# First tiles of a hybrid encoder step: statistics on TensorE, fewer and larger loads, another split of the first h

## The chip, the cores and the metric

The kernel runs on one core of one Trainium2 chip, as one launch that takes every input from device memory and writes every output there. The metric is device time in microseconds (us); lower is better. TensorE (PE) multiplies matrices, VectorE (DVE) and GpSimd (POOL) do elementwise work, ScalarE (ACT) does functions of one operand, and SyncE (SP) issues all DMA transfers of this kernel from one queue.

## The reference

One layer of a streaming encoder over 2048 prompt positions and 32 sample positions, width 1024, in float32. The part that the change touches is its beginning, for the first 512 positions:

```python
cs = jax.nn.silu(c)
mod = (cs @ ada_w[l] + ada_b[l])[:, None, :]
sh1, sc1, gt1, sh2, sc2, gt2 = jnp.split(mod, 6, axis=-1)
h = rmsnorm(x, norm_mix_g[l]) * (1 + sc1) + sh1
p = h @ w_in                      # columns for u, v, q, k, vv, z, a, b
...
x = x + gt1 * (concat(mixer A, mixer B) @ w_out)
h = rmsnorm(x, norm_ffn_g[l]) * (1 + sc2) + sh2
x = x + gt2 * (jnp.square(jax.nn.relu(h @ w_up[l])) @ w_down[l])
y = rmsnorm(x, final_norm_g)
```

`rmsnorm(x, g)` is x times the power -0.5 of (mean of squares over the 1024 channels + 1e-6), times g. There are two condition vectors c (prompt and sample), so `mod` has two columns. Mixer A is a gated MLP over chunks of 128 positions, for whose `v` columns the second stage of the kernel computes a gelu; mixer B is a gated delta rule.

## The kernel before

Channels lie on the 128 partitions, in KT = 8 tiles k; positions lie along the free dimension, in two halves and, in the first half, in two groups g of 512. A float32 product is made of three matmuls: each operand is split into a high part (ACT copies it to a rounded type) and a low part (DVE subtracts), and high*high, low*high and high*low are added in PSUM (`mm3`). `BH[k]`, `BL[k]` are the parts of h; `wh`, `wl` those of a slab of weights (1 MB, loaded as two halves into raw buffers, `slab`). There are two pairs wh/wl, so slab n+2 takes the place of slab n.

**The first stage** is `startup` (L645). It loads c and the eight tiles of x for group 0, squares them on ACT, adds the squares on DVE (`stats`), and makes the row of factors r in `rms_row` (L779): matmuls with a column of ones sum over the partitions (the squares are the loaded weights, 128 positions at a time), DVE scales and adds epsilon, POOL raises to -0.5 with `pow`, PE transposes back into a row over all partitions (in PSUM bank tag "M", one bank), and ACT copies the row to SBUF. Then it goes over k. `ada_first(k)` (L727) loads two transfers of 512 KB of `ada_w` for this tile of channels (ring "ada" of four buffers in the slots 0 to 3), multiplies them with silu(c) in eight small groups of matmuls that end as partial sums on eight rows, copies these to SBUF on ACT, transposes them on PE (two transposes), and adds the four parts and the bias on DVE, one instruction after the other; one more DVE instruction makes a1 = (1+scale)*g. `h_tile` multiplies x by r (DVE, or POOL where k % 3 is 2), applies a1 and the shift (DVE, POOL or ACT by k) and splits the result. Then four heads' z products take this k (`gemm_k`, `mm3` with 512 columns): heads 0, 1 from slab 1, heads 2, 3 from slab 2, each in a PSUM bank over all eight k (bank tags "g", "g", "g", "L").

After the last k, `z_out` (L1038) puts silu(z) of head h into the next buffer of ring "Q" and stores it to `z_d`. Ring "Q" is the halves of the slots 18, 19, 20, in that order: the four heads use 18 low, 18 high, 19 low, 19 high. Then group 1 of x is loaded, summed and turned into h in the same way (`stats(1)`, `h_tile`), and slab 3 (`w_v`, first part) is set going.

**The second stage** is `v_stage` (L936). It first calls `next_slab`, which sets slab 4 (`w_v`, second part) going; then `v_tile` (L953) for the chunks 0 to 3 with slab 3, and for the same chunks with slab 4. A `v_tile` is 24 matmuls of 260 columns into a bank of ring "g" (three banks), then a gelu on ACT into the next buffer of ring "va": (18, 0), (18, 256), (18, 512), (18, 768), (19, 0) and on. The raw buffers of the slabs 1 to 4 are `raws`: the tile `wr0` and slot 6, in turn.

The order of all instructions on all engines is not written by hand: every operation goes into a `Program` (L203) with a cost and its dependencies by memory region, and `schedule` (L239) plays a list schedule over six engines (DMA is one of them) and emits the instructions in the order of their planned starts. Each engine then runs its instructions strictly in that order, and semaphores enforce the dependencies. What has the earlier due GEMM goes first (`due`). `after` in the change adds a dependency to this plan.

At the very end `final` (L1772) calls `rms_row` with three rows of squares for the last group: the sum so far, and those of tiles 6 and 7.

Of the kernel before, what the change touches and what calls it, by code (L numbers as in the profile page):

```python
# [10 lines left out]
AF = mybir.ActivationFunctionType  # L11
ALU = mybir.AluOpType
# [4 lines left out]
P = 128  # L17
D = 1024
KT = 8
# [171 lines left out]
def R(x):  # L191
    return x.ap if isinstance(x, View) else x
# [132 lines left out]
class Kern:  # L325
# [61 lines left out]
    def dma(self, out, in_, n=None):  # L387
# [4 lines left out]
        self.p.op(DMA, max(500, x), lambda: nc.sync.dma_start(out=R(out), in_=R(in_)), [out], [in_], lat=DMA_LATENCY + min(0, x - 500))  # L392

    def mms(self, calls, cost):

        nc = self.nc

        def fn():
            for out, l, r, kw in calls:
                nc.tensor.matmul(R(out), R(l), R(r), **kw)  # L400

        shape = (calls[0][1].shape[0], calls[0][1].n)
        self.p.op(PE, cost, fn, [c[0] for c in calls], [x for c in calls for x in c[1:3]], table=shape)

    def mm(self, out, lhsT, rhs, cost=None, start=True, stop=True, **kw):
        c = cost or 9 + 4 * rhs.n / 2.4
# [130 lines left out]
    def setup(self):  # L537
        sb = self.sbuf
# [20 lines left out]
        rg = self.ring  # L559
        hv = lambda *ss: [(s, lo) for s in ss for lo in (0, HALF)]  # L560
# [84 lines left out]
    def startup(self):  # L645
        i, c = self.i, self.dma
        c(self.craw, i["cT"])
        self.act(self.cs, self.craw, AF.Silu)
        self.fill(self.ones, 1.0, DVE)
        self.fill(self.mhalf, -0.5, DVE)  # L650
        xr = [[8, 9, 10, 11], [4, 5, 7, 12]]
        x = [[self.slot(s, lo, (P, 512)) for s in xr[g] for lo in (0, HALF)] for g in range(2)]
        load = lambda g: [c(x[g][k], self.x_src(0)(k, 512 * g, 512)) for k in range(KT)]
        row = [self.row[:, 512 * g : 512 * g + 512] for g in range(2)]

        def stats(g):
            acc = row[g]
            self.act(acc, x[g][0], AF.Square)
            for k in range(1, KT):
                sq = self.half("E")  # L660
                self.act(sq, x[g][k], AF.Square)
                self.tt(acc, acc, sq, ALU.add, DVE if g == 0 or k % 2 else POOL)
            self.rms_row([acc], 512, acc)
# [7 lines left out]
        stats(0)  # L671
# [12 lines left out]
        for h in range(H):  # L684
            self.z_out(0, 0, h, zs[h])
        load(1)
        stats(1)
        for k in range(KT):
            self.h_tile(0, 1, k, x[1][k], row[1], self.a1, 0)
        self.next_slab()  # L690
        self.consts()

# [34 lines left out]
    def ada_first(self, f, ps):  # L727

        ws = []
        for e in range(2):  # L730
            w = self.new("ada")
            self.dma(w, self.i["ada0"][f, :, 1024 * e : 1024 * e + 1024])
            ws.append(w)
        for e in range(2):
            self.mms([(ps[32 * s : 32 * s + 2, :256], self.cs[:, 4 * e + s, :], ws[e][:, 256 * s : 256 * s + 256],
                       dict(start=(e == 0), stop=(e == 1), tile_position=(0, 32 * s), skip_group_check=True))
                      for s in range(4)], 480)
# [41 lines left out]
    def rms_row(self, acc, w, out):  # L779

        ps = self.bank("M")

        pieces = [min(e, w - P) for e in range(0, w, P)]
        n = len(pieces)
        calls = []
        for c, e in enumerate(pieces):
            for b, a in enumerate(acc):
                calls.append((ps[:, c : c + 1], a[:, e : e + P], self.ones[:, 0:1],
                              dict(start=(b == 0), stop=(b == len(acc) - 1))))
# [465 lines left out]
    def delta_chain(self, hf, h):  # L1255
        c0 = CHUNKS[hf][0]
        nch = len(CHUNKS[hf])
        S = self.S[h]
# [600 lines left out]
```

## Time and profile before

| | us |
|---|---|
| median of 3 runs | 2356.8 |
| lowest, highest | 2352.51, 2358.11 |
| the profiled execution's own time | 2357.03 |
| its span | 2355.2 |

The page of the profile gives shares over the whole span; the timeline lists instructions with start and duration in us (merged where one follows another, with a count), in brackets the idle time of the engine before it and what ended that. PEclk is the TensorE clock that the profile records as granted; 1.00 is full. A row "PEld" is the load of a stationary operand, which overlaps PE.

### The profile page before, as it was taken

The numbers are of one execution on the slowest core, as the hardware profiler recorded it, in microseconds if no ns is written. First come the engines' busy times: TensorE is split into PE (matmuls) and PEld (weight loads), VectorE is DVE, ScalarE is ACT, GpSimd is POOL, SyncE is SP. The second block draws the span as 40 slices with busy tenths as digits, with TensorE's granted clock in tenths as the row PEclk, the third lists the DMA queues.
The fourth block names the chain that finished last, engine by engine and source line by source line (L and its number), as shares of the span: only waits on it lengthen the run. The fifth ranks groups of instructions, "written<-read, shape, count | busy, mean of one in ns | idle before, by whom it ended". The sixth has DMA issues, their size and how long they took to land.

```text
span 2355.2 us, 45713 instructions
## 1 busy us (share of the span) xinstructions
PE 2304.7 (98%) x15888; PEld 2173.7 (92%) x15888; DVE 1667.3 (71%) x3675; ACT 1226.0 (52%) x2818; POOL 597.4 (25%) x827
## 2 busy tenths in 40 slices
PE   7999999999999999999999999999999999999998
PEld 4877878999999888999999999999999999999998
DVE  5556657567665546479999999877667786666775
ACT  4565646456566434366655555664433574334343
POOL 2234421412432322444444434300000050000001
PEclk9999999999999999999999999999999999999999
DMA  9698667466457767887777787998667797666771
GB/s 317 220 316 290 203 190 247 148 182 200 148 168 240 235 213 237 260 268 272 244 239 250 255 281 245 336 321 270 218 210 253 251 297 248 214 220 219 239 230 54
DMA packets 369264, 556.28 MB, mean 236 GB/s; under 512 B 71212, under 2 KB 191424, under 8 KB 369032
## 3 DMA queue, kind: packets, MB, share of 16 engines
q1 hardware_dynamic: 369032, 553.35, 72.0%
q8 instruction: 126, 2.06, 0.4%
q14 instruction: 106, 0.87, 0.1%
HBM read 398.92 MB, written 154.28 MB: 235 GB/s over the span
## 4 chain that ended last, share of the span: by engine, by line
PE 83%; DMA 6%; DVE 6%; ACT 3%; issue 2%; POOL 1%; SPq 0%; POOLq 0%; DVEq 0%; ACTq 0%
PE f L400 50%; PE g L400 24%; PE C L400 3%; DVE s L354 2%; ACT s L339 2%; PE B L400 2%; PE L L400 1%; DVE s L359 1%; DMA pk_d<-s 1%; DVE wl L354 1%; DMA s<-ada 1%; PE M L400 1%; PE L L411 1%; DVE BL L354 1%; DMA s<-xT 1%
## 5 line engine op out<-in xcount | busy, mean ns | idle before, releaser
L339 ACT ACTIVATE s<-s 128x348 fp32r<-128x348 f32 (+13 forms) x1079 | 494.8, 482 | 348.0 <-DVE s L354 136.3
L400 PE MATMUL f<-s,wh 128*128 128x348 f32 (+1 forms) x2760 | 661.4, 322 | 5.8 <-DVE s L359 2.4
L400 PEld LDWEIGHTS f<-s,wh 128*128 128x128 f32 x2760 | 479.4, 188 | 9.2 <-DVE s L354 3.5
L354 DVE TENSOR_TENSOR s<-f,s 128x348 f32<-128x348 f32 (+1 forms) x696 | 347.6, 511 | 179.3 <-PE f L400 178.3
L400 PE MATMUL f<-s,wl 128*128 128x348 f32 (+1 forms) x1380 | 443.6, 321 | 0.3 <-DVE wl L354 0.3
L400 PE MATMUL g<-BH,wh 128*128 128x512 f32 (+2 forms) x1112 | 422.6, 380 | 2.0 <-ACT BH L339 2.0
L354 DVE TENSOR_TENSOR s<-s,s 128x348 fp32r<-128x348 f32 (+7 forms) x688 | 356.0, 545 | 58.1 <-ACT s L339 24.1
L400 PE MATMUL g<-BH,wl 128*128 128x512 f32 (+2 forms) x1112 | 392.6, 353 | 0.0
L400 PE MATMUL g<-BL,wh 128*128 128x512 f32 (+2 forms) x1112 | 391.3, 352 | 0.2 <-DVE BL L354 0.2
L400 PE MATMUL f<-BL,wh 128*128 128x348 f32 (+1 forms) x1016 | 328.9, 324 | 2.2 <-DVE BL L354 2.2
L400 PE MATMUL f<-BH,wh 128*128 128x348 f32 (+1 forms) x1016 | 328.3, 323 | 1.7 <-ACT BH L339 1.7
L400 PE MATMUL f<-BH,wl 128*128 128x348 f32 (+1 forms) x1016 | 328.5, 323 | 0.0
L339 ACT ACTIVATE wh<-s 128x512 fp32r<-128x512 f32 (+1 forms) x278 | 174.0, 634 | 236.2 <-PE f L400 189.5
L354 POOL TENSOR_TENSOR s<-s,s 128x512 f32<-128x512 f32 (+5 forms) x154 | 188.7, 1233 | 304.0 <-ACT s L339 148.2
L354 POOL TENSOR_TENSOR s<-s 64x39 f32<-64x39 f32 (+12 forms) x299 | 156.7, 524 | 426.7 <-issue 381.0
L400 PEld LDWEIGHTS f<-s,wl 128*128 128x128 f32 x1380 | 259.8, 188 | 0.7 <-DVE wl L354 0.6
L400 PEld LDWEIGHTS g<-BH,wh 128*128 128x128 f32 x1112 | 211.3, 190 | 26.0 <-issue 7.8
L400 PEld LDWEIGHTS g<-BH,wl 128*128 128x128 f32 x1112 | 210.3, 189 | 19.4
L400 PEld LDWEIGHTS g<-BL,wh 128*128 128x128 f32 x1112 | 211.5, 190 | 15.2 <-DVE BL L354 0.6
L354 DVE TENSOR_TENSOR wl<-s,wh 128x512 fp32r<-128x512 f32 (+1 forms) x278 | 211.2, 768 | 19.2 <-ACT wh L339 18.9
L359 DVE SCALAR_TENSOR_TENSOR s<-s,s,s 128x128 f32<-128x128 f32 (+5 forms) x318 | 163.5, 529 | 71.9 <-ACT s L339 43.8
L354 DVE TENSOR_TENSOR wl<-wr,wh 128x512 fp32r<-128x512 f32 (+2 forms) x161 | 153.5, 956 | 63.9 <-ACT wh L339 61.1
(115 smaller groups left out, 3400.5 us busy)
## 6 DMA issues: line engine op xcount, KB each, us to landing
s<-w_u SPq DMA_DIRECT2D x124, 256.0 KB, 3.8
s<-w_d SPq DMA_DIRECT2D x118, 256.0 KB, 2.8
wh<-su_d SPq DMA_DIRECT2D x113, 256.0 KB, 3.1
wl<-su_d SPq DMA_DIRECT2D x113, 256.0 KB, 4.2
wh<-sd_d SPq DMA_DIRECT2D x108, 256.0 KB, 3.1
wl<-sd_d SPq DMA_DIRECT2D x108, 256.0 KB, 3.9
wr<-w_b SPq DMA_DIRECT2D x42, 512.0 KB, 4.7
s<-adaw SPq DMA_DIRECT2D x32, 512.0 KB, 5.7
```

Source lines behind the costliest of these rows:

```text
L339: self.p.op(ACT, c, lambda: nc.scalar.activation(out=R(out), in_=R(in_), func=func, **{k: R(v) for k, v in kw.items()}), [out, accum], [in ...
L354: self.p.op(eng, c, lambda: e.tensor_tensor(out=R(out), in0=R(a), in1=R(b), op=op), [out], [a, b])
L359: self.p.op(DVE, c, lambda: nc.vector.scalar_tensor_tensor(out=R(out), in0=R(a), scalar=R(s), in1=R(b), op0=op0, op1=op1), [out], [a, s, b])
L400: nc.tensor.matmul(R(out), R(l), R(r), **kw)
L411: self.p.op(PE, 114, lambda: nc.tensor.transpose(R(out), R(in_), R(ident)), [out], [in_, ident])
```

## The change

It alters the first stage, one shared helper and one later load:

- x comes in four transfers of 512 KB per group instead of eight of 256 KB.
- For group 0, all eight squares are kept (new ring "sq", in the slots 14, 15, 21, 22) and `rms_row` gets them as a list. `rms_row` now makes one PE operation per row of squares instead of one for all; for a single row this is what it was. DVE adds no squares for group 0, and r stays in PSUM and is read there.
- One `pow` on POOL is issued ahead of everything, its result unused.
- In `ada_first`, two matmuls with a 128x2 matrix `sel` of ones and zeros take the place of the two transposes, and sum the four parts; one DVE instruction adds the bias. `sel` is made with three DVE instructions.
- For group 0, h is made by DVE (x*r), ACT (scale and shift), and the split; POOL has no part in it.
- Ring "ada" has eight buffers: the slots 0, 1, 2, 3, 25, 26, 27, 20. `after` keeps the matmuls of `ada_first(k)` behind the GEMMs of k-3 in the plan.
- `raws` gets slots 18 and 19, ahead of slab 1: slab 1 now uses wr0 and slot 6, slab 2 slots 18 and 19, slab 3 wr0 and slot 6, slab 4 slots 18 and 19.
- The load of the sample's delta state s0, which the plan had put first of all, is kept behind the last k.

```diff
@@ setup
+        self.sel = sb("sel", [P, 2])
-        rg("ada", [(s, 0) for s in range(4)], (P, 1024))
+        rg("ada", [(s, 0) for s in (0, 1, 2, 3, 25, 26, 27, 20)], (P, 1024))
+        rg("sq", hv(14, 15, 21, 22), (P, 512))
@@ startup
+        both = [[self.slot(s, 0, (P, 2, HALF))[:, :, :512] for s in xr[g]] for g in range(2)]
+        load = lambda g: [c(both[g][e], i["xT"][2 * e : 2 * e + 2, :, 512 * g : 512 * g + 512].rearrange("k p t -> p k t"),
+                            8 * P * 512) for e in range(4)]
+        row = self.row[:, :512]
+        def stats():
+            sq = [self.half("sq") for _ in range(KT)]
+            for k in range(KT):
+                self.act(sq[k], x[0][k], AF.Square)
+            return self.rms_row(sq, 512, None)
+        self.tt(self.rcol[0], self.ones[:, :4], self.mhalf, ALU.pow, POOL)
         load(0)
...
+        self.tt(self.sel, self.ident[:, 0:2], self.ident[:, 32:34], ALU.add)
+        for e in (64, 96):
+            self.tt(self.sel, self.sel, self.ident[:, e : e + 2], ALU.add)
+        r = stats()
         self.sq = self.slab_list()
+        self.raws += [self.slot(s, 0, (P, SLABW // 2)) for s in (18, 19)]
         self.sn = self.slab(*self.sq.pop(0))
...
+        done = []
         for k in range(KT):
-            self.ada_first(k, ps[k % 2])
-            self.h_tile(0, 0, k, x[0][k], row[0], self.a1, 0)
+            self.ada_first(k, ps[k % 2], done[k - 3] if k > 2 else ())
+            t = x[0][k]
+            self.tt(t, t, r, ALU.mult)
+            self.act(t, t, AF.Identity, scale=self.a1[:, k, 0:1], bias=self.modc[:, 0, k, 0:1])
+            self.split(self.BH[k][:, :512], self.BL[k][:, :512], t)
             for h in range(H):
                 self.gemm_k(zs[h][:, :512], *z[h // 2], h % 2, 0, 0, k)
+            done.append((len(self.p.ops) - 1,))
+        self.begun = done[-1]
@@ ada_first
-            self.tr(ps[:, 256 + 128 * e : 384 + 128 * e], ar[:, 128 * e : 128 * e + 128], self.ident)
+            self.mm(ps[:, 256 + 2 * e : 258 + 2 * e], ar[:, 128 * e : 128 * e + 128], self.sel, 230)
         m = self.modc[:, 0:2, f]
-        for s in range(4):
-            part = ps[:, 256:512].re("p (e s r) -> p e s r", e=2, s=4)[:, :, s, 0:2]
-            self.tt(m, part, self.adab[:, 0:2, f] if s == 0 else m, ALU.add)
+        self.tt(m, ps[:, 256:260].re("p (e r) -> p e r", e=2), self.adab[:, 0:2, f], ALU.add)
@@ rms_row
-        self.mms(calls, 230 * len(calls))
+        for b, a in enumerate(acc):
+            self.mms([(ps[:, c : c + 1], a[:, e : e + P], self.ones[:, 0:1],
+                       dict(start=(b == c == 0), stop=(b == len(acc) - 1 and c == n - 1), skip_group_check=len(acc) > 1))
+                      for c, e in enumerate(pieces)], 230 * n)
@@ delta_chain
-                self.dma(S, self.i["s0"][h])
+                self.dma(S, self.i["s0"][h], after=self.begun)
```

The statistics of group 1 keep their old form, with the additions on DVE and POOL in turn.

More of the change, by code (lines that the diff above doesn't have):

```diff
@@ L385, in transpose32, with dma @@
         self.p.op(DVE, 68 + 1.042 * out.n, lambda: nc.vector.transpose(R(out), R(in_)), [out], [in_])
-    def dma(self, out, in_, n=None):
+    def dma(self, out, in_, n=None, after=()):
         nc = self.nc
@@ L391, in dma, with mms @@
         x = b / 360
-        self.p.op(DMA, max(500, x), lambda: nc.sync.dma_start(out=R(out), in_=R(in_)), [out], [in_], lat=DMA_LATENCY + min(0, x - 500))
-    def mms(self, calls, cost):
+        self.p.op(DMA, max(500, x), lambda: nc.sync.dma_start(out=R(out), in_=R(in_)), [out], [in_], lat=DMA_LATENCY + min(0, x - 500), after=after)
+    def mms(self, calls, cost, after=()):
         nc = self.nc
@@ L402, in mms @@
         shape = (calls[0][1].shape[0], calls[0][1].n)
-        self.p.op(PE, cost, fn, [c[0] for c in calls], [x for c in calls for x in c[1:3]], table=shape)
+        self.p.op(PE, cost, fn, [c[0] for c in calls], [x for c in calls for x in c[1:3]], table=shape, after=after)
     def mm(self, out, lhsT, rhs, cost=None, start=True, stop=True, **kw):
@@ L652, in startup @@
         x = [[self.slot(s, lo, (P, 512)) for s in xr[g] for lo in (0, HALF)] for g in range(2)]
[L653 to L663, printed above, removed]
+        both = [[self.slot(s, 0, (P, 2, HALF))[:, :, :512] for s in xr[g]] for g in range(2)]
[8 more added lines that the diff above has]
+        self.tt(self.rcol[0], self.ones[:, :4], self.mhalf, ALU.pow, POOL)
         load(0)
@@ L670, in startup @@
         self.cp(self.ident, k1[:, 120:248])
-        stats(0)
+        self.tt(self.sel, self.ident[:, 0:2], self.ident[:, 32:34], ALU.add)
+        for e in (64, 96):
+            self.tt(self.sel, self.sel, self.ident[:, e : e + 2], ALU.add)
+        r = stats()
         self.sq = self.slab_list()
+        self.raws += [self.slot(s, 0, (P, SLABW // 2)) for s in (18, 19)]
         self.sn = self.slab(*self.sq.pop(0))
@@ L686, in startup @@
         load(1)
-        stats(1)
+        self.act(row, x[1][0], AF.Square)
+        for k in range(1, KT):
+            sq = self.half("E")
+            self.act(sq, x[1][k], AF.Square)
+            self.tt(row, row, sq, ALU.add, DVE if k % 2 else POOL)
+        self.rms_row([row], 512, row)
         for k in range(KT):
-            self.h_tile(0, 1, k, x[1][k], row[1], self.a1, 0)
+            self.h_tile(0, 1, k, x[1][k], row, self.a1, 0)
         self.next_slab()
@@ L725, in consts, with ada_first @@
                 self.dma(self.pk_d[h][8][:, :, :P], zero.re("p (a b) -> p a b", a=3))
-    def ada_first(self, f, ps):
+    def ada_first(self, f, ps, after=()):
         ws = []
@@ L736, in ada_first @@
                        dict(start=(e == 0), stop=(e == 1), tile_position=(0, 32 * s), skip_group_check=True))
-                      for s in range(4)], 480)
+                      for s in range(4)], 480, after)
         ar = self.arow[:, 256 * (f % 2) : 256 * (f % 2) + 256]
@@ L784, in rms_row @@
         n = len(pieces)
[L785 to L789, printed above, removed]
-        self.mms(calls, 230 * len(calls))
+        for b, a in enumerate(acc):
+            self.mms([(ps[:, c : c + 1], a[:, e : e + P], self.ones[:, 0:1],
+                       dict(start=(b == c == 0), stop=(b == len(acc) - 1 and c == n - 1), skip_group_check=len(acc) > 1))
+                      for c, e in enumerate(pieces)], 230 * n)
         r = self.rcol[0]
```

## Prediction, made before the changed kernel ran

> **What bounds the kernel now.** I read the page first, then the timeline of PE over the first 62 us, then that of the other engines, then the windows in which the clock fell.
>
> ```profile
> span 2355.2 us, 45713 instructions
> PE 2304.7 (98%) x15888; PEld 2173.7 (92%) x15888; DVE 1667.3 (71%) x3675; ACT 1226.0 (52%) x2818; POOL 597.4 (25%) x827
> ```
>
> ```profile
> 12.64 1.87 PE L400 MATMUL M<-ones,s 128*128 128x1 f32 x8 [12.64 <-DVE s L354]
> 14.44 2.17 PE L400 MATMUL C<-s,s 128*2 128x256 f32 x16
> 16.78 1.12 PE L411 MATMUL M<-ident,rcol 128*128 128x128 f32 x4 [0.17 <-POOL rcol L354]
> ...
> 24.18 1.03 PE L400 MATMUL C<-s,s 128*2 128x256 f32 x8 [1.75 <-DMA s<-ada]
> 25.15 0.80 PE L400 MATMUL g<-BH,wh 128*128 128x512 f32 x1
> ...
> 40.68 0.61 PE L400 MATMUL C<-s,s 128*2 128x256 f32 x8 [0.56 <-DMA s<-ada]
> ...
> 43.47 0.38 PE L411 MATMUL C<-ident,s 128*128 128x128 f32 x2
> ...
> 56.52 0.95 PE L400 MATMUL M<-ones,s 128*128 128x1 f32 x8
> ...
> 58.81 0.28 PE L400 MATMUL g<-wh,BH 128*128 128x260 f32 x1
> ...
> 60.11 0.28 PE L400 MATMUL g<-wl,BH 128*128 128x260 f32 x1
> 61.31 0.65 PE L411 MATMUL M<-ident,rcol 128*128 128x128 f32 x4 [0.92 <-POOL rcol L354]
> ```
>
> PE is busy for 2304.7 of 2355.2 us, so only 50 us of the span can be had without taking work off PE, and 12.64 of these lie ahead of PE's first instruction; the first z product starts at 25.15. From there PE stands still once for 0.56 us, until an `ada` load has landed, and the second stage begins at 58.81. Of the 33.7 us in between, nearly all is PE work. So three questions decide: when does the first z product start, how much PE work follows it, and does the second stage still start to run without a gap?
>
> ```profile
> 4.44 1.40 ACT L339 ACTIVATE s<-s 128x512 f32<-128x512 f32 x2 [1.34 <-DMA s<-xT]
> 7.24 3.95 ACT L339 ACTIVATE s<-s 128x512 f32<-128x512 f32 x6 [1.40 <-DMA s<-xT]
> 11.91 0.68 DVE L354 TENSOR_TENSOR s<-s,s 128x512 f32<-128x512 f32 x1
> 14.79 1.94 POOL L354 TENSOR_TENSOR rcol<-rcol,mhalf 128x4 f32<-128x4 f32 x1 [13.22 <-DVE rcol L368]
> 18.57 0.69 DVE L354 TENSOR_TENSOR s<-s,s 128x512 f32<-128x512 f32 x1
> ```
>
> ```profile
> 3.00:10.00 7.00, 0.00 (x0) 0.00 (x0) 2.58 (x4) 4.05 (x8) 0.00 (x0) 1.00 0.98 334
> ```
>
> The last row is a window (start:end, length, busy time and count of five engines, granted clock, DMA share, GB/s). Now the squares end at 11.19, the sum on DVE at 12.59, and r is first used at 18.57.
>
> **The change part by part.**
>
> *Loads of x.* From 3 to 10 us the DMA engines are busy 0.98 of the time at 334 GB/s (last two columns): issuing half as many transfers gains nothing there. What goes is the s0 issue ahead of them, and a pair of tiles now lands together:
>
> ```profile
> 0.73 0.41 SPq L392 DMA_DIRECT2D s<-s  x1
> ```
>
> One issue is 0.46 us apart from the next, and a second tile of 256 KB needs 0.78 us at 334 GB/s: the first pair lands at 4.44 - 0.46 + 0.78 = 4.8, and its first square (0.66, six in 3.95) ends at 5.4. The last two squares still end near 11.
>
> *Squares summed by PE.* Each tile now costs PE eight instructions. The trace has two prices: 14.44 - 12.64 = 1.80 us at 12.64, and 0.95 us at 56.52. The first is at half the clock, the second at the full one. Eight tiles: 14.4 or 7.6 us. So the sum ends at 5.4 + 14.4 = **19.8** if PE stays cold, and at about 15.4 if its clock comes up once it has been busy for a while (two or three tiles cold, the rest at 0.95). With the DVE it was 14.51. In both cases PE, not the last square at 11, sets the end. What raises the clock is read from these windows (second column PE busy, third from last the granted clock; ahead of its first record the column says 1.00, though the rows at 12.64 and 14.44 ran at half speed):
>
> ```profile
> 13.92:17.33 3.41, 3.13 (x22) 1.27 (x23) 1.30 (x2) 0.62 (x2) 1.94 (x1) 1.00 0.93 370
> 24.16:27.57 3.41, 3.39 (x15) 2.05 (x16) 2.81 (x8) 0.38 (x1) 0.73 (x1) 0.50 1.01 408
> ...
> 2341.81:2345.22 3.41, 2.59 (x22) 2.42 (x20) 0.97 (x4) 0.98 (x2) 0.00 (x0) 1.00 0.00 0
> 2345.22:2348.63 3.41, 1.20 (x5) 0.71 (x5) 1.14 (x4) 0.00 (x0) 0.86 (x1) 0.50 0.00 0
> ...
> 1034.52:1037.93 3.41, 1.51 (x9) 1.19 (x10) 3.41 (x6) 2.17 (x5) 2.50 (x2) 1.00 1.06 395
> 1037.93:1041.34 3.41, 3.41 (x13) 2.98 (x12) 3.41 (x5) 2.16 (x5) 2.63 (x3) 0.50 0.91 290
> ```
>
> At the very end, a window with PE busy for 2.59 of 3.41 us, most of it this same one-column kind of matmul, was followed by half the clock. I take that as a sign that such matmuls do not hold the clock up, and choose 19.8; 15.4 is a rival.
>
> The Trainium skill, "TensorE: Matmul & The Clock Gate", Part 1, says that the clock comes up after one busy window of about 3.4 us. By that rule alone PE, busy from 5.4 on, would be warm from its second window and the sum would end at about 15.4. The closing windows above speak against counting these matmuls as busy.
>
> *The early power.* The first `pow` takes 1.94, the second 1.02:
>
> ```profile
> L354 POOL TENSOR_TENSOR rcol<-rcol,mhalf x4: 1018/1024/1937, 14.8 to 189.5; 128x4 f32<-128x4 f32 x4
> ```
>
> I take 1.02 here; it runs while PE does the two groups of `ada_first(0)` (2.17 us cold). If the early one does not help, 0.92 more is still inside that cover, nearly.
>
> *From the sum to the first product.* 19.8, then the matmuls of `ada_first(0)`, whose data have landed long before, 2.17: 22.0. Four transposes of r, 1.12: 23.1. The two `sel` matmuls are four instructions of the kind at 12.64, 0.22 each: 24.0. One DVE addition and a1, with the waits between them 0.6: 24.6. The x*r of DVE (0.69) is done by then. ACT's scale and shift and the high part follow:
>
> ```profile
> 33.89 0.81 ACT L339 ACTIVATE s<-s,modc,a 128x512 f32<-128x512 f32 x1 [1.82 <-DVE a L368]
> 34.88 0.62 ACT L339 ACTIVATE BH<-s 128x512 fp32r<-128x512 f32 x1
> ```
>
> 24.6 + 0.81 + 0.62 + 0.1 = **26.1**, 1.0 later than now. With the warm sum: 15.4 + 1.1 + (pow) 1.3 + 0.65 + 0.5 + 0.6 + 1.5 = 20.4 or so, 4.8 earlier. The work taken from POOL and the three additions taken from DVE lie on other engines; that they are quicker is in these sums already.
>
> *PE work behind it.* Now six of sixteen groups of `ada_first` run ahead of 25.15 (16, 16, 8 and 8 instructions at 14.44 to 24.18); with the sums in front I expect four, two more groups of 0.61 stay behind: +1.2. Four `sel` instructions at 0.12 (0.95/8) against 0.38 for two transposes, at seven k: +0.7. The wait of 0.56 goes, as eight buffers let the loads run ahead: -0.6. So the second stage starts 1.0 + 1.3 = **2.3 later** (warm: 4.8 - 1.3 + 1.2 for a cold window of 3.41 us saved, 4.7 earlier).
>
> *Slab 4 in slots 18 and 19.* This is the part that I weigh most. Now slab 4 is loaded into wr0 and slot 6, which are free once slab 3 is split, and nothing in slot 18 waits for it:
>
> ```profile
> 58.44 1.07 ACT L339 ACTIVATE s<-g 128x512 f32<-128x512 f32 x2
> ...
> 60.03 0.33 SPq L392 DMA_DIRECT2D s<-w_v  x1
> ...
> 64.78 0.38 ACT L339 ACTIVATE s<-g 128x256 f32<-128x256 f32 x1
> ...
> 66.46 1.08 ACT L339 ACTIVATE wh<-s 128x1040 fp32r<-128x1040 f32 x1 [0.34 <-DMA s<-w_v]
> 66.55 1.23 DVE L354 TENSOR_TENSOR wl<-wr,wh 128x1040 fp32r<-128x1040 f32 x1
> ```
>
> After the change its first half must wait until the stores of heads 0 and 1 have left slot 18; and the gelu of chunk 0 writes (18, 0), so it must wait until that half is loaded and split. That is a new chain of five steps. It takes, in the times of now: silu of head 1 ends at 58.98; store to landing 5.2 (3.6 to 6.8, below); load 5.7; high part 1.08; low part 1.23; gelu 0.38 and 0.5 for the waits between: 73.1.
>
> ```profile
> L392 SPq DMA_DIRECT2D z_d<-s x4: 326/348/442, 56.6 to 61.8; - x4
> ...
> DMA to landing us min/median/max: 3.6/5.2/6.8
> ```
>
> ```profile
> wr<-w_b SPq DMA_DIRECT2D x9, 512.0 KB, 5.7
> ```
>
> Meanwhile PE has three banks. (60.11 - 58.81)/11 = 0.118 us per matmul, 2.84 per `v_tile`: three are done at 67.3, and the fourth needs the bank that gelu 0 empties. PE waits 5.8 us. Now it waits 0.92 in this stretch, for `pow` (with the start of the next, 1.1), which falls into the same wait: **+4.7** net. With the shortest store and a load of 4.7 it is 2.1, with the longest and the 6.4 of the load at 60.03 it is 7.0. No other PE work is ready: the chunks 4 to 7 need h of group 1, the next block of conditioning a buffer in slot 7, where x of group 1 lies. And at 1034.52 a window with half of it idle was followed by 3.41 us at half the clock, so **+1.7** on top (0 to 3.4).
>
> *The end.* `rms_row` for the last group:
>
> ```profile
> 2343.17 0.49 ACT L339 ACTIVATE s<-s 128x344 f32<-128x344 f32 x1 [0.50 <-DVE s L359]
> 2343.71 1.81 PE L400 MATMUL M<-ones,s 128*128 128x1 f32 x14 [0.61 <-ACT s L339]
> ```
>
> 14 instructions follow the last square; three columns of two are needed, the other eight can go earlier: 8 x 1.81/14 = **-1.0**. Nothing covers this chain, so it counts in full.
>
> *At no cost.* s0, first read in the delta stage, is issued later, in a queue with room. The three instructions that make `sel` run while DVE, which adds no squares any more, has nothing else.
>
> **Sum**, on the profiled execution's own 2357.03: +2.3 + 4.7 + 1.7 - 1.0 = +7.7, **2364.7**. That execution is 0.2 above the median, which I leave.
>
> **The rivals.**
>
> 1. *Clock up during the sum*: the start 4.7 earlier, the wait for slot 18 as above: -4.7 + 6.4 - 1.0 = +0.7, 2357.7. For it: PE is occupied without a gap; against it: the closing windows.
> 2. *It does what it says*: the sum follows the squares at 0.95 per tile and ends near 13, the first product starts near 18.5, so the second stage 6.6 earlier; and the wait for slot 18 is short or planned around, the wait of 1.1 gone: -6.6 - 1.1 - 1.0 = -8.7, 2348. It needs a warm PE from the start, which no row shows.
> 3. *Cold sum, but no wait at slot 18* (the plan finds PE other work): +2.3 - 1.1 - 1.0 = +0.2, 2357.
> 4. *A different order far behind*: the plan is made anew from shifted times. PE waits little in the whole span now; a store or a chain that slips adds to the 7.7, say by the longest prices above (7.0 and 3.4): +11.7, 2369 and beyond.
>
> **How the numbers follow.** Within 0.3% (7 us, about what a measurement of this kernel can tell from no change) lies 2349.7 to 2363.9. My forecast has 0.48, of which 0.37 are above the upper bound, as its own range with the bounds of the two waits is 2360 to 2371; rival 1 has 0.18, 2 has 0.16, 3 has 0.07, 4 has 0.11. Slower: 0.37 + 0.11 = 0.48. Same: 0.11 + 0.18 + 0.07 + 0.01 = 0.37. Faster: 0.15, nearly all of rival 2. The range 2349 to 2372 leaves out most of rival 2 and the far end of 4.
>
> **What would show it.** In the profile after: the M matmuls from about 5.4, eight tiles up to 19.8 at 1.80 each (rival 1 and 2: 0.95); the first z product at 26; the second stage at 61; then three tiles of it, a PE wait of some 6 us ended by ACT or a freed bank, with the `w_v` load into slot 18 landing just before, and PEclk 0.50 behind it; 6 matmuls instead of 14 after the last square. I am wrong if the gelu of chunk 0 comes within three tiles of the second stage's start, or if the first z product starts before 21.

## The result, and the profile after

| | before | after |
|---|---|---|
| median, us | 2356.72 (6 runs) | 2369.73 (6 runs) |
| lowest, highest, us | 2352.51, 2358.11 | 2367.11, 2374.38 |
| the profiled execution, us | 2357.03 | 2374.38 |
| ratio of after to before | | 1.0061, 95% interval 1.0050 to 1.0071 |

The changed kernel is slower by 0.61%, some 14 us (13.0 by the medians). Its profiled execution is the slowest of its six, 4.7 us above the median, so its rows stand for a rather long execution; where that matters, other kernels are put beside it.

The page after, its span and its busy time:

```profile
span 2372.6 us, 45838 instructions
...
PE 2322.8 (98%) x15960; PEld 2192.6 (92%) x15960; DVE 1666.6 (70%) x3645; ACT 1231.1 (52%) x2822; POOL 593.9 (25%) x824
```

PE is busy 18.1 us longer (2322.8 against 2304.7), while the span grew by 17.4. The idle time did not grow (49.8 against 50.5): PE's first instruction comes 6.1 earlier, and a new wait of 5.12 takes that up. So the loss stands in the profile as busy time, though only 72 instructions were added: the same kinds of instructions take longer. The timeline of PE shows where (start, duration, instruction, count, idle time ahead of it and what ended that):

```profile
6.53 13.81 PE L400 MATMUL M<-ones,s 128*128 128x1 f32 x64 [6.53 <-ACT s L339]
20.27 1.89 PE L400 MATMUL C<-s,s 128*2 128x256 f32 x16
...
23.78 1.89 PE L400 MATMUL C<-s,s 128*2 128x256 f32 x16
27.04 1.02 PE L400 MATMUL C<-sel,s 128*128 128x2 f32 x4 [1.38 <-ACT s L339]
27.98 1.89 PE L400 MATMUL C<-s,s 128*2 128x256 f32 x16
29.80 0.80 PE L400 MATMUL g<-BH,wh 128*128 128x512 f32 x1
...
36.06 1.04 PE L400 MATMUL C<-s,s 128*2 128x256 f32 x16
...
64.61 0.28 PE L400 MATMUL g<-wh,BH 128*128 128x260 f32 x1
...
67.02 0.65 PE L411 MATMUL M<-ident,rcol 128*128 128x128 f32 x4 [0.82 <-POOL rcol L354]
...
80.01 0.59 PE L400 MATMUL g<-wh,BH 128*128 128x260 f32 x1 [5.12 <-ACT s L339]
```

The 64 one-column matmuls begin with the first squares at 6.53 and run back to back until 20.27, 1.72 us for each tile of x. Behind them the sixteen conditioning instructions of one slab of `ada_w` take 1.89, which is the half-clock price; those at 36.06 are the first at 1.04, so all twelve matmuls of the first four z products (29.80 to 35.9) ran at half clock. The first z product starts at 29.80 (before: 25.15), the second stage at 64.61 (before: 58.81), and after three of its tiles PE stands still for 5.12 us. What that gap waits for is read from the timelines of SP's queue and of ACT:

```profile
68.63 1.75 SPq L392 DMA_DIRECT2D s<-w_v  x2
```

```profile
75.19 1.07 ACT L339 ACTIVATE wh<-s 128x1040 fp32r<-128x1040 f32 x1 [1.19 <-DMA s<-w_v]
...
78.28 1.28 ACT L339 ACT_TABLE_LOAD   x1
79.57 0.94 ACT L339 ACTIVATE s<-g 128x256 f32<-128x256 f32 x3
```

The load of slab 4 is issued at 68.63, the split waits for it until 75.19, a table load takes 1.28, and the gelus that empty the banks come at 79.57, three in a row. The windows show the clock (start:end, length, busy time and count of five engines, granted clock, DMA share, GB/s):

```profile
6.53:20.27 13.74, 13.74 (x64) 13.72 (x65) 2.02 (x6) 4.97 (x8) 0.41 (x2) 1.00 1.02 394
...
80.00:90.00 10.00, 9.99 (x69) 9.99 (x70) 6.52 (x14) 7.16 (x20) 0.94 (x2) 0.81 0.43 127
```

In the first row PE is busy for all of 13.74 us and still at half speed, as its durations show (the column says 1.00 until the trace has its first clock record). Behind the gap the clock is low again: a mean of 0.81 over 10 us is 3.8 us at half, worth 1.9 us. At the very end of the kernel:

```profile
2358.14 0.80 PE L400 MATMUL M<-ones,s 128*128 128x1 f32 x6 [0.17 <-DVE s L354]
2358.80 0.72 PE L400 MATMUL f<-s,s 128*128 128x344 f32 x3
...
2361.98 0.83 PE L400 MATMUL M<-ones,s 128*128 128x1 f32 x6 [1.31 <-ACT s L339]
```

Six instead of fourteen matmuls follow the last square, but the two early sums now stand among the last tile's own matmuls (the `f` rows).

### The profile page after: what moved, and what is told of

Same layout as the page of the kernel before. It is cut to its first block, busy times and chain, and to the rows that moved or that the text cites. A ratio compares the mean times of both kernels' runs of the same rounds, so it can differ in the third digit from the quotient of the medians.

```text
span 2372.6 us, 45838 instructions
## 1 busy us (share of the span) xinstructions
PE 2322.8 (98%) x15960; PEld 2192.6 (92%) x15960; DVE 1666.6 (70%) x3645; ACT 1231.1 (52%) x2822; POOL 593.9 (25%) x824
## 4 chain that ended last, share of the span: by engine, by line
PE 45%; DVE 4%; issue 1%; DMA 1%; ACT 1%; POOL 0%; POOLq 0%; DVEq 0%; SPq 0%; ACTq 0%
PE f L400 45%; DVE s L354 2%; DVE wl L354 1%; DVE s L359 1%; DMA s<-th_d 0%; ACT s L339 0%; DVE BL L354 0%; POOL s L354 0%; DMA s<-w_d 0%; DMA su_d<-wh 0%; ACT wh L339 0%; PE M L400 0%; DMA su_d<-wl 0%; POOL wr L354 0%; PE M L411 0%
## 5 line engine op out<-in xcount | busy, mean ns | idle before, releaser
L400 PEld LDWEIGHTS f<-s,wh 128*128 128x128 f32 x2760 | 479.7, 188 | 10.6 <-DVE s L354 4.3
L354 DVE TENSOR_TENSOR s<-s,s 128x348 fp32r<-128x348 f32 (+8 forms) x675 | 352.7, 553 | 43.3 <-ACT s L339 20.3
L339 ACT ACTIVATE wh<-s 128x512 fp32r<-128x512 f32 (+2 forms) x280 | 176.3, 637 | 241.2 <-PE f L400 202.6
L354 POOL TENSOR_TENSOR s<-s,s 128x512 f32<-128x512 f32 (+4 forms) x152 | 189.3, 1253 | 293.6 <-ACT s L339 160.1
L354 DVE TENSOR_TENSOR wl<-s,wh 128x512 fp32r<-128x512 f32 (+2 forms) x280 | 215.9, 779 | 22.1 <-ACT wh L339 21.9
L359 DVE SCALAR_TENSOR_TENSOR s<-s,s,s 128x400 f32<-128x400 f32 (+5 forms) x318 | 162.4, 527 | 59.4 <-ACT s L339 31.6
```

The source lines that it names most:

```text
L339: self.p.op(ACT, c, lambda: nc.scalar.activation(out=R(out), in_=R(in_), func=func, **{k: R(v) for k, v in kw.items()}), [out, accum], [in ...
L354: self.p.op(eng, c, lambda: e.tensor_tensor(out=R(out), in0=R(a), in1=R(b), op=op), [out], [a, b])
L359: self.p.op(DVE, c, lambda: nc.vector.scalar_tensor_tensor(out=R(out), in0=R(a), scalar=R(s), in1=R(b), op0=op0, op1=op1), [out], [a, s, b])
```

## The experiments

Twelve kernels ran. Each ratio is to the kernel before, on the same chip. Repeats of one kernel lie up to 13 us apart, so terms of 1 or 2 us are read from the traces.

| kernel | median, us | before, us | ratio (95% interval) |
|---|---|---|---|
| slab 4 as before | 2363.51 | 2355.24 | 1.0039 (1.0024 to 1.0054) |
| squares added on DVE | 2361.02 | 2355.24 | 1.0033 (1.0021 to 1.0046) |
| both | 2356.33 | 2355.24 | 1.0010 (1.0000 to 1.0020) |
| no early power | 2367.94 | 2355.24 | 1.0056 (1.0041 to 1.0071) |
| warm sum | 2369.48 | 2355.73 | one run |
| both, row sum as one operation | 2353.82 | 2355.73 | 0.9994 (0.9985 to 1.0003) |
| both, conditioning held back | 2365.45 | 2355.73 | 1.0038 (1.0024 to 1.0051) |
| both, held back, one operation, warm start | 2364.80 | 2355.73 | 1.0036 (1.0024 to 1.0049) |
| both, one operation, warm start | 2356.41 | 2353.83 | 1.0010 (1.0000 to 1.0021) |
| before, slab 4 in slots 18, 19 | 2362.43 | 2353.83 | 1.0039 (1.0023 to 1.0056) |
| before, row sum in parts | 2354.72 | 2353.83 | 1.0004 (0.9994 to 1.0014) |
| both, one operation, third slab held back | 2356.00 | 2353.98 | 1.0004 (0.9995 to 1.0014) |

### Slab 4 as before

```diff
         z = [self.next_slab(), self.sn]
+        self.raws = self.raws[:2]
```

> The changed kernel, but slab 4 is loaded into wr0 and slot 6 again (slots 18 and 19 only for slab 2). Theory: the 5.1 us wait of PE at 74.7 to 80 goes, with the 1.9 us lost to the half clock behind it: 6 to 7 us faster than the changed kernel's 2369.7, about 2363; PE has no wait over 1.2 us between 62 and 90. Rival (h of group 1, not slot 18, sets the second stage): the wait only moves, 2368 to 2370.

The wait is gone (the longest of PE from 62 to 90 us is the 0.82 for `rcol`), the first product (29.65) and the second stage (64.29) stay late, and about a third of the loss goes.

### Squares added on DVE

```diff
         def stats():
-            sq = [self.half("sq") for _ in range(KT)]
-            for k in range(KT):
-                self.act(sq[k], x[0][k], AF.Square)
-            return self.rms_row(sq, 512, None)
+            self.act(row, x[0][0], AF.Square)
+            for k in range(1, KT):
+                sq = self.half("sq")
+                self.act(sq, x[0][k], AF.Square)
+                self.tt(row, row, sq, ALU.add)
+            return self.rms_row([row], 512, None)
```

> The changed kernel, but the squares of group 0 are added on DVE again (one row to the sum on PE); all else stays. Theory: the sum ends near 14.5 instead of 20.3, the first product starts near 24.5 instead of 29.8, the second stage 5 to 6 us earlier: about 2364, with the wait at slot 18 still there. Rival (the six groups of the conditioning that the plan puts ahead of the first product set its start): first product still at 28 or later, 2368 or more.

The timeline of PE in this kernel:

```profile
12.54 1.86 PE L400 MATMUL M<-ones,s 128*128 128x1 f32 x8 [12.54 <-DVE s L354]
...
23.85 0.80 PE L400 MATMUL g<-BH,wh 128*128 128x512 f32 x1
...
57.65 0.28 PE L400 MATMUL g<-wh,BH 128*128 128x260 f32 x1
...
72.26 0.41 PE L400 MATMUL g<-wh,BH 128*128 128x260 f32 x1 [4.27 <-ACT s L339]
```

With eight one-column matmuls instead of 64, the sum ends near 14.3 instead of 20.27, the first product comes 6.0 earlier and the second stage 7.0 earlier, while the gap at slab 4 stays. Its time is some 3 us under the expected, about what its interval reaches to one side; but the second stage also moved by 7.0 where 5 to 6 were expected, so the start cost more than the prediction gave it.

### Both undone

The two edits above together.

> Both of these: squares of group 0 added on DVE, slab 4 in wr0 and slot 6; larger transfers, early power, eight buffers, selection matrix, h by two engines stay. Theory: the two losses add: 2357 to 2358, no different from before within 0.1%. If the other parts gain something, up to 3 us less; if there is a third loss, 2360 or more.

The two parts add up: from 1.0061 the edits alone take off 0.22 and 0.28%, both together 0.51%. They hold five sixths of the loss.

### No early power

The line that issues the `pow` ahead of everything is left out.

> The changed kernel without the early power. Theory, from the trace after (the early power takes 1.02, as does the one at 20.69): nothing is warmed up; the power at 20.7 still takes 1.02 and the time stays at 2369.7 within the noise (0.1%). The reason given for it: the power at 20.7 takes 1.9 again; as it runs beside 1.8 us of matmuls, the time would grow by 0.5 us at most.

The one that counts still takes 1.02 us, in the timeline of POOL:

```profile
19.95 1.02 POOL L354 TENSOR_TENSOR rcol<-rcol,mhalf 128x4 f32<-128x4 f32 x1 [12.81 <-DVE rcol L368]
```

So an earlier `pow` does not shorten it, and the 1.94 of before was not the price of being the first. In the trace of before that `pow` (14.79 to 16.73) ran beside a DVE instruction with two inputs (14.63, 1.23 us). The same holds in the two kernels that keep the first stage of before ("Slab 4 in slots 18 and 19, alone" and "The row sum in parts, alone"): 1.94 both times, beside the same DVE instruction. In the kernels with the change's first stage that instruction has ended before the `pow`, which takes 1.02. No run moves this one instruction alone, so it is the likely reason, not a shown one. The time (1.0056 against 1.0061) can't be told from that of the changed kernel.

### Warm sum

Twelve full matmuls, whose result nothing reads, are put ahead of the sum in the changed kernel.

```diff
         self.tt(self.rcol[0], self.ones[:, :4], self.mhalf, ALU.pow, POOL)
+        wu = self.bank("L")
+        self.mms([(wu[:, :P], self.ones, self.ones, dict(start=True, stop=True, skip_group_check=True))] * 12, 5000)
```

> The changed kernel with twelve 128x128x128 float32 matmuls of `ones` by `ones` into a free bank, ahead of the squares' sum; nothing reads their result. They fill TensorE from about 1 to 6 us with real matmuls. Theory (the sum is slow because the clock is at half, and one-column matmuls, unlike full ones, do not keep the clock up): the first M groups run at about 0.95 us per eight, then, one or two clock windows after the last full matmul, 1.72 to 1.8 again; the sum ends at 16 to 18 instead of 20.3. Rival A (one-column matmuls keep the clock up once it is up): all eight groups at 0.95 where their squares are there, the end at 13.5 to 14, and the conditioning behind it at full clock. Rival B (the price of 1.72 us is not the clock's): every group 1.72 again, the end at 20.3 or later.

The timeline of PE in this kernel (a float32 matmul is recorded as two instructions), and two windows:

```profile
1.05 5.49 PE L400 MATMUL L<-ones 128*128 128x128 f32 x24 [1.05 <-DVE mhalf L381]
6.32 10.65 PE L400 MATMUL M<-ones,s 128*128 128x1 f32 x64
16.91 1.89 PE L400 MATMUL C<-s,s 128*2 128x256 f32 x16
...
26.44 0.80 PE L400 MATMUL g<-BH,wh 128*128 128x512 f32 x1
```

```profile
7.40:10.80 3.40, 3.40 (x31) 3.40 (x31) 0.60 (x4) 2.97 (x6) 0.06 (x1) 0.94 1.01 352
10.80:14.20 3.40, 3.40 (x17) 3.40 (x17) 1.21 (x3) 1.16 (x2) 0.00 (x0) 0.50 1.02 419
```

This separates the three accounts of the expectation. In the first window 31 instructions are done, at a clock of 0.94; in the second 17, at 0.50, with PE busy for the whole of both. So the price of a one-column matmul is the clock's (rival B falls), and such matmuls, back to back, let the clock drop some 4 us after the last full matmul (rival A falls). The sum ends at 16.91, within the 16 to 18 expected. The Trainium skill, "TensorE: Matmul & The Clock Gate", Part 1, has the clock come up after one sustained busy window of some 3.4 us; for these matmuls the trace disagrees, with 13.74 us of unbroken busy time at half speed in the changed kernel and a clock that falls while PE is busy here. The measurement decides: PE that is busy with such matmuls alone is not brought to full clock, nor kept there. The first product comes 3.4 us earlier than in the changed kernel and the second stage 4.1 (60.49); this kernel's one time, 2369.48, says nothing on what that is worth.

### The row sum as one operation

Both parts undone, and `rms_row` hands its matmuls to the planner as one operation again. Within it they still go square by square, as in the change; in the kernel before they go column by column.

```diff
-        for b, a in enumerate(acc):
-            self.mms([(ps[:, c : c + 1], a[:, e : e + P], self.ones[:, 0:1],
-                       dict(...))
-                      for c, e in enumerate(pieces)], 230 * n)
+        self.mms([(ps[:, c : c + 1], a[:, e : e + P], self.ones[:, 0:1],
+                   dict(...))
+                  for b, a in enumerate(acc) for c, e in enumerate(pieces)], 230 * n * len(acc))
```

> The kernel with both parts undone (squares added up on VectorE, slab 4 loaded in its old place) with the row sum issued as one TensorE operation again instead of one for each square. Theory (the planner put the two early part sums of the tail between the last tile's matmuls, and that cost what the shorter last sum saved): in the last tile no M matmul before the last square, 6 x the pieces behind it in one go, and from the first transpose of the last tile to the scale of its row 13.0 to 13.5 us instead of 14.8; the kernel 1 to 2 us under the one with both parts undone, some 2355. Rival (the tail's length is set by the squares on ScalarE, wherever the sums stand): 14.5 to 14.9 us, and the same time within 0.5 us.

The end of the kernel, in the timelines of PE and DVE:

```profile
2332.82 0.49 PE L411 MATMUL M<-ident,rcol 128*128 128x128 f32 x3
...
2343.55 2.31 PE L400 MATMUL M<-ones,s 128*128 128x1 f32 x18
```

```profile
2345.89 0.16 DVE L368 TENSOR_SCALAR rcol<-M 128x3 f32<-128x3 f32 x1 [1.44 <-PE M L400]
```

Twelve of the 18 one-column matmuls stand ahead of the wait for the last square, six behind it, and none between the last tile's own matmuls. From 2332.82 to 2345.89 are 13.07 us; the same stretch is 15.42 in the kernel with both parts undone alone (2329.24 to 2344.66; its last six matmuls fell into half clock, 1.44 instead of 0.83), 14.83 after and 14.05 before. This is the only version whose median lies under that of before, by 1.9 us, but the interval reaches from 3.5 faster to 0.7 slower: it cannot be called faster.

It shows something else. Up to the end its instructions stand in the same order as in the kernel with both parts undone, and yet its second stage starts 2.7 us later. The timeline of PE with both parts undone, then with the row sum as one operation as well:

```profile
23.45 0.80 PE L400 MATMUL g<-BH,wh 128*128 128x512 f32 x1
...
24.48 0.48 PE L400 MATMUL g<-BH,wl 128*128 128x512 f32 x1
...
55.84 0.28 PE L400 MATMUL g<-wh,BH 128*128 128x260 f32 x1
```

```profile
23.72 0.80 PE L400 MATMUL g<-BH,wh 128*128 128x512 f32 x1
...
29.99 1.15 PE L400 MATMUL C<-s,s 128*2 128x256 f32 x16
...
58.51 0.28 PE L400 MATMUL g<-wh,BH 128*128 128x260 f32 x1
```

In the first the clock comes up one us after the first product, in the second some six after it. The second stage differs by 2.67 us, of which 0.27 are there at the first product. The Trainium skill, "TensorE: Matmul & The Clock Gate", Part 1, says that the window runs freely, so that the cold stretch varies from run to run; that it varies is what these two executions show. One execution can't price a start to better than that.

### The row sum in parts, alone

The kernel before with the change's form of `rms_row`; only the end differs from before.

> The kernel before with the row sum issued as one operation for each square, as in the change; only the last group's end differs from the kernel before. Theory (early sums between the last tile's matmuls cost more than the shorter last sum saves): from the transposes of the group before (2331.51 in the kernel before) to the scale of the last row 14.8 to 15.5 us instead of 14.05, the kernel 0.8 to 1.4 slower, 2356.5. Rival (as predicted, eight of fourteen matmuls go earlier at no cost): 13.0 and 1.0 faster.

The end in the timeline of PE of this kernel:

```profile
2341.19 0.80 PE L400 MATMUL M<-ones,s 128*128 128x1 f32 x6 [0.16 <-DVE s L354]
2341.85 0.72 PE L400 MATMUL f<-s,s 128*128 128x344 f32 x3
...
2345.02 0.83 PE L400 MATMUL M<-ones,s 128*128 128x1 f32 x6 [1.31 <-ACT s L339]
```

From the transposes of the group before (2331.08) to the scale of the row (2345.88) are 14.80 us against 14.05. The early sums delay the last tile's matmuls, and with them the residual sum on DVE and the last square; as theory had it. The time (1.0004) is too coarse for 0.75 us.

### Slab 4 in slots 18 and 19, alone

The kernel before with one line of the change.

```diff
         self.sq = self.slab_list()
+        self.raws += [self.slot(s, 0, (P, SLABW // 2)) for s in (18, 19)]
```

> The kernel before with one line of the change alone: slots 18 and 19 join the raw buffers, so that slab 4 loads there. Theory (the load has to wait for the z stores, the first gelu for the load, and TensorE for the gelu's bank): three tiles of the second stage, then a wait of TensorE of 4 to 6 us ended by ScalarE, half clock behind it, and a time of 2360 to 2363. Rival (the plan alone did it, and without the rest of the change it finds other work): no wait over 1.2 us in the second stage, 2355 to 2358.

The start of the second stage and its wait, in the timeline of PE of this kernel:

```profile
60.26 0.37 PE L400 MATMUL g<-wh,BH 128*128 128x260 f32 x1
...
76.64 0.59 PE L400 MATMUL g<-wh,BH 128*128 128x260 f32 x1 [7.35 <-ACT s L339]
```

The wait comes without any other part of the change, and is longer than expected (7.35). The whole kernel loses 0.39%, some 9 us.

### Holding the conditioning back

Both undone, and the plan's limit made tighter:

```diff
-            self.ada_first(k, ps[k % 2], done[k - 3] if k > 2 else ())
+            self.ada_first(k, ps[k % 2], done[k - 2] if k > 1 else ())
```

> The kernel with both parts undone, with the conditioning of the third slab held back behind the first slab's second transformation (the limit that the change removed, for that slab alone). Theory (the plan's order put six groups of conditioning ahead of the first z product): the first z product at about 21.5 to 22 instead of 23.45, the second stage 0.5 to 1.5 us earlier than 55.84. Rival (TensorE's work is only moved; the loads set what follows): the first product is earlier and the second stage starts at 55.5 to 56.2 as before.

The expectation describes the edit wrongly: it holds back every slab from the third on, and the kernel before had no such limit. Both theories missed. The first product came 7.65 us behind the end of the sum instead of 9.52, which is the price of the group; but in this execution the sum began 1.1 later (13.24), so the product was only 0.8 earlier (22.68). PE then ran out of conditioned slabs. The timeline of PE, from the sum of the second group of positions to the second stage:

```profile
56.26 1.70 PE L400 MATMUL M<-ones,s 128*128 128x1 f32 x8 [1.00 <-DVE a L368]
...
65.72 0.28 PE L400 MATMUL g<-wh,BH 128*128 128x260 f32 x1
```

PE waited 0.58 us at 34.9, and 0.69 and 1.00 us at 53.8 and 56.3; behind the last two the clock fell (eight M instructions in 1.70), and products of the first stage ran at half until 63. The second stage starts 9.9 us later than in the kernel with both parts undone (55.84), 7.2 later than in the one with the row sum as one operation (58.51). The kernel that joins this limit with the row sum as one operation and a warm start (34 full matmuls, whose result nothing reads, as under "Warm start" below) is late as well:

> Both parts undone, the row sum as one operation, the third slab's conditioning held back, and 34 full matmuls of `ones` ahead of the conditioning, whose result nothing reads. Theory: TensorE is at full clock from about 5 us, the conditioning and the first z products take half as long, the second stage starts at about 53 instead of 55.84, and the kernel takes 2350 to 2353. Rival (the start waits on loads and on the other engines, not on TensorE): the second stage stays at 55 to 56 and the time at 2355 to 2357.

Its second stage starts at 61.83, later than without either. So the lookahead of three slabs that the change allows is needed somewhere behind the start. With the third slab alone held back (`done[max(k - 3, 0)] if k > 1`), and without the warm start:

> The kernel with both parts undone and the row sum as one operation, with the third slab's conditioning alone held back behind the first slab's four products (all later limits as in the change). Theory (one cold conditioning group stands ahead of the first product, and the limit of one slab for every slab was what starved TensorE later): the first product at 21.5 to 22.7 instead of 23.72, that group at about 1.0 us instead of 1.89, no wait of TensorE over 1 us from there to the second stage, which starts at 54.5 to 56; the kernel about 1 us under the one without the limit, 2352.5. Rival (holding a group back starves the later slabs here too): second stage at 60 or later and the time over 2358.

The timeline of PE in this kernel:

```profile
21.94 0.77 PE L400 MATMUL g<-BH,wh 128*128 128x512 f32 x1
...
27.93 1.91 PE L400 MATMUL C<-s,s 128*2 128x256 f32 x32
...
59.09 0.37 PE L400 MATMUL g<-wh,BH 128*128 128x260 f32 x1
```

The first product and the price of the group came as theory had it (7.64 behind the sum instead of 9.52; 32 instructions in 1.91, so 0.95 for sixteen), and no wait behind the first product is over 1 us. But the second stage is no earlier: 59.09, against 58.51 in the execution without this limit, which ran its first products at half clock too. What the order gained was lost again: PE waits 2.15 us for ACT ahead of the first product and 0.62 later on for the low part of an h, and the four transposes of the second row now stand ahead of the second stage (0.35). Both theories missed the second stage; the rest of the difference was not followed.

### Warm start

Both undone, the row sum as one operation, and 34 full matmuls from 1 us on, whose result nothing reads.

> The kernel with both parts undone and the row sum as one operation, with 34 full matmuls of `ones` by `ones` (result unused) from 1 us on, and the limit on the conditioning as in the change. Theory: the first stage was short of TensorE's clock; with the clock up from about 5 us the conditioning groups ahead of the first product take 1.0 us each instead of 1.9, the first products 0.23 instead of 0.43 apart, and the second stage starts at 52 to 54 instead of 55.8 (58.5 in the execution without the 34); the kernel takes 2349 to 2352. Rival (loads and the other engines set the start): second stage at 55 to 58, time 2353 to 2355.

The timeline of PE in this kernel:

```profile
17.27 0.61 PE L400 MATMUL C<-s,s 128*2 128x256 f32 x8 [0.62 <-DMA s<-ada]
...
21.09 1.89 PE L400 MATMUL C<-s,s 128*2 128x256 f32 x16
22.91 0.80 PE L400 MATMUL g<-BH,wh 128*128 128x512 f32 x1
```

At full clock the groups take 0.61 for eight instructions, and three of the first four wait for their `ada` load (0.56, 0.62 and 0.67 us); in the same order without the 34, at half clock, PE loses some 0.3 us to these loads (2.15 instead of 1.89 for sixteen). After these waits the clock falls again, by 20 us, and the first product comes at 22.91, only 0.8 earlier than without the 34; the second stage starts at 56.51. The second stage is where the rival had it, between the 55.84 and the 58.51 of the same order without the 34; the time is above both ranges, and 1.0010 can't be told from no change. What a faster PE gained here went into waits for loads, and into the half clock behind them.

## Why the prediction was right and wrong

It said slower, 2364.7 us in a range of 2349 to 2372; measured were 2369.73. The sign, and the two mechanisms that carry most of the loss, were right; the loss was 13.0 us by the medians instead of 7.7. Some terms agree only because errors cancel. Term by term:

**Cold sum: right, its end in part by luck.** 1.80 us a tile and the end at 19.8 were predicted, 1.72 and 20.27 measured. The sum began 1.1 later than forecast (6.53 instead of 5.4, as the first pair of tiles landed late: its first square starts at 5.85, not 4.8), and the lower price a tile made up for 0.6 of that. The warm sum showed that the clock sets the price, and that these matmuls do not hold it up; the closing windows that the choice was based on could not show that, since PE was also idle for a quarter of the first of them. Rivals 1 and 2, which had the clock up during the sum, fall.

**From the sum to the first product: the step that failed.** Before, this stretch takes 10.6 us (14.51 to 25.15). Predicted were 6.3 (19.8 to 26.1), measured 9.53 (20.27 to 29.80). I had priced one slab's conditioning there (2.17), though I expected two to stand ahead of the first product; three stand there, as many as before, each at half clock. What else went wrong is in the timelines of DVE and ACT after:

```profile
24.52 1.21 DVE L354 TENSOR_TENSOR wl<-s,wh 128x1024 fp32r<-128x1024 f32 x1
25.64 0.23 DVE L368 TENSOR_SCALAR a<-modc,nrm 128x2 f32<-128x2 f32 x1
```

```profile
25.91 0.81 ACT L339 ACTIVATE s<-s,modc,a 128x512 f32<-128x512 f32 x1 [2.35 <-DVE a L368]
26.62 0.36 ACT L339 ACTIVATE s<-C 128x256 f32<-128x256 f32 x1
26.89 0.62 ACT L339 ACTIVATE BH<-s 128x512 fp32r<-128x512 f32 x1
```

The plan put the low part of a slab on DVE (1.21) ahead of a1, and on ACT the copy for the second slab behind the scale of the first h. So the high part of h was ready at 27.5, not at 26.1; PE waited 1.38 for that copy, and then did the third slab's group before the product, whose operand had been ready for 2.3 us. The sum in the prediction follows the data alone; every engine also runs what the plan put in between. The two kernels above with the sum on DVE and the same plan behind it show the same stretch, 9.52 each time.

**From the first product to the second stage: right by luck.** 33.66 (58.81 - 25.15, as before) + 1.3 were predicted, 34.81 measured. The two groups of eight conditioning instructions that were to be moved behind the first product (+1.2) were not, since six of sixteen groups stood ahead of it as before. In their place came the clock: twelve matmuls ran at half instead of four (each 0.43 us apart instead of 0.23, so 1.6 us). Before, the clock is up by the sixth:

```profile
27.74 0.39 PE L400 MATMUL g<-BH,wl 128*128 128x512 f32 x1
```

So the term "second stage 2.3 later" became 5.8. Undoing the sum gave back 0.28%, some 6.6 us.

**Slab 4: right, in mechanism and nearly in size.** Predicted were a wait of 5.8, with the 0.92 for `rcol` falling into it (+4.7 net), and 1.7 for the clock. Measured: a wait of 5.12, half clock for 3.8 us behind it (1.9 us), and the wait for `rcol`, 0.82, still there, since it comes ahead of the gap and not within it; that is +5.0 net, and 1.9. Within the chain errors cancel: the load was issued 3.9 us after the silu of head 1 (5.2 priced), took up to 6.6 (5.7), and 4.4 instead of 2.8 passed from the split to the gelu, as ACT's table load of 1.28 was not in the sum. Undoing it gave back 0.22%, some 5 us, with an interval of about 4 to each side; alone on the kernel before it cost 0.39%, some 9 us. Rival 3 falls.

**The end: wrong.** Predicted -1.0, measured 14.83 against 14.05, +0.8. "The other eight can go earlier" took their place for free; they went between the last tile's matmuls. With the sums in one piece the stretch is 13.07, which is the -1.0.

**Early power: no price either way,** as the prediction allowed; its cover was not needed.

Two sums of the prediction do not come out as written: the warm first product adds up to 21.05, not 20.4, which puts rival 1 at 2358.4; and the upper end of its own range by its terms is 2369 (2.3 + 7.0 + 3.4 - 1.0), not 2371. Neither changes what was forecast.

Rival 4 named the region where the time fell, 2369 and beyond, but not the cause: it was to be a new order far behind, and what was found lies in the first 90 us and at the end. The rows above give 5.8 + 6.9 + 0.8 = 13.5, and the medians 13.0. The profiled execution after lost 3.8 us more in between (at the transposes ahead of the last tile it is 16.5 late, 2348.02 against 2331.51); these were not traced, and that execution is 4.7 above its kernel's median. Of the 0.61%, the two parts hold 0.51; the rest is within what the end (0.8 us) and the intervals can hold. Loads of x in pairs, the selection matrix, the split of h and the eight `ada` buffers, together and with the end repaired, came to 0.9994: nothing that can be told from no change.

## What to carry to other kernels

PE busy is not PE warm: before a sum over partitions is moved to matmuls with a column of ones, look in the trace for what the clock did behind such matmuls, and price them cold if nothing else runs beside them. An extra buffer is only a gain if its next reader and its last writer are both off the path; here the gelu's own target was lent to a load, and PE paid for the store, the load and the split. Where a planner orders the work, an operation that is split or freed early goes where the plan likes, and it may be ahead of what the end waits for.

## What the hardware showed that was not expected

64 one-column matmuls, 13.74 us without a gap, never brought the clock up, and some 4 us of them took it down from full (0.94, then 0.50). The same order of instructions ran its first products at full speed after one us in one execution and after some six in another, worth 2.4 of the 2.67 us by which their second stages differ. Without an earlier one, the first `pow` of a launch took 1.02 us; the 1.94 of before was seen in three kernels, each time beside a DVE instruction with two inputs.
